# Inputs laid out in reading order, shift and scale columns summed on VectorE, and a first block by k-tiles

## The chip, the cores and the metric

The kernel runs on one core of a Trainium2 chip. The core has five engines that work side by side, each in the order of its own instruction list: TensorE for matrix products (PE in the profile; PEld is its weight load), VectorE (DVE), ScalarE (ACT), GpSimd (POOL) and SyncE (SP), which here only issues transfers. Data come from device memory (HBM) by DMA into the on-chip memory SBUF; matrix products are written to PSUM. The metric is the device time of one execution in microseconds.

## The reference

The program is a small conditioned decoder with two layers on a sequence of 256 positions of width 1024. Each layer is a feed-forward half step, an attention, and another feed-forward half step. In front of every sub-layer stands a normalisation with a shift and a scale, and behind it a gate, that all come from the vector `c`. Cut to what matters here:

```python
c_act = silu(c)
for layer in range(2):
    mods = c_act @ ada_w[layer] + ada_b[layer]          # (1024) x (1024, 9216)
    sh1, sc1, g1, sh2, sc2, g2, sh3, sc3, g3 = split(mods, 9)
    h = rms_norm(x, norm_g[layer, 0]) * (1 + sc1) + sh1
    x = x + 0.5 * g1 * ((silu(h @ w_gate) * (h @ w_up)) @ w_down)    # 1024 -> 2816 -> 1024
    h = rms_norm(x, norm_g[layer, 1]) * (1 + sc2) + sh2
    x = x + g2 * attention(h)             # layer 0: moba, layer 1: mla with its own pair "kv"
    h = rms_norm(x, norm_g[layer, 2]) * (1 + sc3) + sh3
    x = x + 0.5 * g3 * swiglu(h, ...)
```

There are 20 vectors of 1024 from `c` that serve as shift, scale or gate of the two layers and of the pair "kv". Each is a product of `c_act` with a 1024 x 1024 matrix of 4 MB. All data are float32.

## The kernel before, in words

The 256 positions are two tiles `t` of 128 partitions; the width 1024 is eight k-tiles of 128. For a matrix product the normalised `x` is transposed on PE, so that the width lies on the partitions. A shift or scale is then one number per partition, a column of `m_cols`; a gate is wanted along the free dimension, as a row repeated on all partitions.

**Products.** Almost every product is made of three, in a faster format (`mm3`, L695 to L697): both operands are split into a rounded part and a rest, `hi` by ACT (L505) and `lo` by DVE (L506), 1024 columns at a time. A weight tile `raw` of 1 MB (three buffers) is loaded by SP (`wload`, L673), split into `hi` and `lo` (eight buffers each), and its buffer is free when both have read it. Rows of a transfer are as the weights lie in memory: 1 KB for tiles of gate and up, 2 KB for down.

**Vectors from c.** 18 of the 20 vectors are streamed beside the rest (`ada_vec`): eight tiles `adaw` of 128 rows and 1024 columns each (three buffers, L517), and for each tile DVE multiplies with a number per partition and adds into `acc` (L518). POOL clears `acc` beforehand and loads the bias into its row 0. In the end `acc` has to be summed over its 128 partitions. For a gate that is a product with ones (L537, L538). For a shift or scale (12 vectors) `col_sums` transposes `acc` on PE, four blocks of 128 into one PSUM bank `adaps` (L529), and DVE reduces the bank along its rows into four columns (L564); for a scale one more small DVE instruction adds 1 and multiplies the gain (L558). How far the stream runs is set by paces: five vectors are issued during the first feed-forward, one in the first attention, six in the second feed-forward, five in the third, one in the last.

**First block.** The first two vectors, shift and scale of the first sub-layer, are needed at once, so `first` makes the first 512 columns of gate and up with unsplit float32 products (L1527) while the vectors arrive. It works in five rounds of 128, 256, 256, 256 and 128 columns of the vectors. A round loads both vectors' columns for all eight k-tiles (L1445) and the weights of its one or two k-tiles (L1454), forms the columns (round 0 by 32 small products on PE, the others by DVE accumulation, L1488, and products with ones), scales and shifts the transposed `x` on ACT and does the products. The split form of the result is kept for the other blocks.

**Order.** The program is first written down in a sequence with waits for the dependencies; then the class `Order` plays it through with a cost for each instruction and sets each engine's order by need, with numbers for the transfer rate and latency (`RATE`, and the two sums with 1400 and 300 ns). PE's instructions on `adaps` go ahead of others there. On the chip each engine runs its list strictly in that order, and an instruction whose data are late holds all behind it. `first_rank` gives ranks for the first block; `held` keeps some side work (tables for the attention bias) back until 34 us.

Of the kernel before, what the change touches and what calls it, by code (L numbers as in the profile page):

```python
# [68 lines left out]
FFN_PACE = 172.0  # L69

ROUNDS = (128, 256, 256, 256, 128)

INS = ["x", "c", "positions", "ada_w", "ada_b", "norm_g", "ffn_w_gate", "ffn_w_up",
       "ffn_w_down", "rel_bias", "moba_w_qkv", "moba_q_g", "moba_k_g", "moba_w_o",
       "kv_ada_w", "kv_ada_b", "kv_norm_g", "w_dkv", "kv_a_norm_g", "w_uk", "w_uv",
       "mla_k_g", "mla_w_dq", "mla_q_a_norm_g", "mla_w_uq", "mla_q_g", "mla_w_o"]
# [13 lines left out]
RATE = 392.0  # L90
# [55 lines left out]
class Order:  # L146
# [114 lines left out]
    def place(self, need):  # L261
# [70 lines left out]
        while placed < n:  # L332
# [86 lines left out]
def trunk(ctx: ExitStack, tc: tile.TileContext, a: dict, out: bass.AP):  # L419
# [69 lines left out]
    c_rows = tp.tile([P, 256], F32, tag="y", name="c_rows", bufs=4)[:KD, :P]  # L489
    nc.sync.dma_start(c_rows, a["c"].rearrange("o (k p) -> (o k) p", p=P))  # L490
    cact = cp.tile([P, KD], F32, name="cact")
    pos_f = a["positions"].rearrange("o s -> (o s)")
    for t in range(NT):
        nc.scalar.dma_start(xs[t], a["x"][0, t * P:(t + 1) * P, :])
    NGAIN = 7 * KD
    NROW = NGAIN + 2 * KD
    g_rows = cp.tile([P, P], F32, name="g_rows")
    g_cols = cp.tile([P, NROW], F32, name="g_cols")
    m_cols = cp.tile([P, 2, NGAIN], F32, name="m_cols")

# [8 lines left out]
    def ada_vec(w, b, col, finish, rows):  # L509


        acc = adap.tile([P, D], F32, tag="acc", name=nm("acc"), bufs=2)
        nc.gpsimd.memset(acc, 0.0)  # L513
        nc.gpsimd.dma_start(acc[0:1, :], b[col:col + D].rearrange("(o n) -> o n", o=1))
        for k in range(KD):
            wt = adap.tile([P, D], F32, tag="adaw", name=nm("adaw"))
            nc.sync.dma_start(wt, w[k * P:(k + 1) * P, col:col + D])  # L517
            nc.vector.scalar_tensor_tensor(acc, wt, cact[:, k:k + 1], acc,  # L518
                                           op0=ALU.mult, op1=ALU.add)
            if k < KD - 1:  # L520
                yield
        if rows:
            ahi, alo = split(acc, D)

        def col_sums():
            for hh in range(2):
                pt = ps_ada.tile([P, 512], F32, tag="ada", name=nm("adaps"))
                for j in range(4):
                    nc.tensor.transpose(kslice(pt, j), kslice(acc, 4 * hh + j), ident)  # L529
                pe(0.44)  # L530
                finish(hh, pt)

        def sums():
            for hh in range(2):
                pt = ps_ada.tile([P, 512], F32, tag="ada", name=nm("adaps"))
                sl = slice(hh * 512, (hh + 1) * 512)
                nc.tensor.matmul(pt, ones_r, ahi[:, sl], start=True, stop=False)  # L537
                nc.tensor.matmul(pt, ones_r, alo[:, sl], start=False, stop=True)  # L538
                pe(0.44)
                finish(hh, pt)  # L540
        later(3.0, sums if rows else col_sums)
        yield

    mods = {}
    ready = set()

    def mod(*key):
        until(lambda: key in ready)
        return mods.get(key)

    MOD_KEYS = [(0, 0), (0, 1), (0, 2), (1, 0), (1, 1), (1, 2), "kv"]

    def col_slice(t, key, k0=0, n=KD):
        c0 = MOD_KEYS.index(key) * KD + k0
        return t[:, c0:c0 + n]

    def scale_col(ps, key, k0=0, n=KD):
        nc.vector.scalar_tensor_tensor(col_slice(m_cols[:, 1, :], key, k0, n), ps, 1.0,  # L558
                col_slice(g_cols, key, k0, n), op0=ALU.add, op1=ALU.mult)

    def col_fin(key, i):
        def fin(hh, pt):
            s = small([P, 4], "acol") if i else col_slice(m_cols[:, 0, :], key, 4 * hh, 4)
            nc.vector.tensor_reduce(s, pt.rearrange("p (k q) -> p k q", q=P), axis=AX.X, op=ALU.add)  # L564
            if i:
                scale_col(s, key, 4 * hh, 4)
            if hh:
                ready.add((key, ("sh", "sc")[i]))
        return fin

    def gate_fin(key, mul):
        t = mods[key, "g"] = modp.tile([P, D], F32, tag="gate", name=nm("gate"))

        def fin(hh, pt):
            nc.scalar.activation(t[:, hh * 512:(hh + 1) * 512], pt, AF.Copy, scale=mul)
            if hh:
                ready.add((key, "g"))
        return fin

    def ada_items():  # L580
        for layer in range(2):
            w, b = a["ada_w"][layer], a["ada_b"][layer]
            for sub in range(3):
                if layer == 1 and sub == 1:
                    yield a["kv_ada_w"], a["kv_ada_b"], 0, lambda: col_fin("kv", 0), False
                    yield a["kv_ada_w"], a["kv_ada_b"], D, lambda: col_fin("kv", 1), False
                key = (layer, sub)
                if key != (0, 0):
                    yield w, b, 3 * sub * D, lambda key=key: col_fin(key, 0), False
                    yield w, b, (3 * sub + 1) * D, lambda key=key: col_fin(key, 1), False  # L590
                yield (w, b, (3 * sub + 2) * D,
                       lambda key=key: gate_fin(key, 1.0 if key[1] == 1 else 0.5), True)

    def ada_stream():
        for w, b, col, fin, rows in ada_items():
            yield from ada_vec(w, b, col, fin(), rows)
# [21 lines left out]
    def wsrcs():  # L618
        for layer in range(2):
            for idx in range(2):  # L620
                wg, wu, wd = (a[n][layer, idx] for n in ("ffn_w_gate", "ffn_w_up", "ffn_w_down"))
                if (layer, idx) != (0, 0):
                    for w in (wg, wu):
                        for k0 in range(0, KD, 4):
                            yield w[k0 * P:(k0 + 4) * P, :FB], 4, FB
                for f0 in range(FB, F, S):
                    for w in (wg, wu):
                        yield w[:, f0:f0 + S], KD, S
                for half in range(2):
                    for k0 in range(0, KF, 4):  # L630
                        kt = min(4, KF - k0)
                        yield wd[k0 * P:(k0 + kt) * P, half * 512:(half + 1) * 512], kt, 512
                if idx == 1:
                    continue
                if layer == 0:
                    wqkv = a["moba_w_qkv"][0]
                    for g in (0, -1, 1, 2, -2, 3):
# [953 lines left out]
```

## Time and profile before

| what | us |
|---|---|
| median of three runs | 1100.16 |
| lowest and highest run | 1097.55, 1102.19 |
| profiled execution | 1093.43 |
| its span from the first to the last instruction | 1091.7 |
| PE, DVE, ACT busy in the span | 1030.6, 810.1, 583.1 |
| moved by DMA | 260.66 MB, 239 GB/s in the mean |

In the lines of the profile, times are microseconds and `L529` is a line of the kernel. A group of instructions is given as line, engine, operation, result<-operands with their shapes, a count, then the time busy in total and the mean of one in nanoseconds, and then how long the engine stood idle just before them and what ended that. A wait is given as engine and line that waited, what it waited for, the total time, the number of waits and the longest. A line of the timeline is start, duration, engine, line, operation; in square brackets stands the idle time before it. "issue" is a wait that the profile couldn't assign. The duration of an instruction contains the time in which its result travels, so that the next one can start before the end; what one instruction costs its engine is the distance of two starts.

### The profile page before, as it was taken

What the parts mean: (1) busy time and instruction counts of PE and PEld (TensorE: products, weight loads), DVE (VectorE), ACT (ScalarE), POOL (GpSimd) and SP (SyncE); (2) the same over time, 40 slices, a digit from 0 to 9 for tenths busy, and PEclk for the clock granted to TensorE, in tenths of its full rate; (3) what the DMA queues carried; (4) which work ended last, traced back from release to release, by engine and by line L of the source; (5) the groups of instructions that cost most, each with busy time, mean ns of one, the idle gap of its engine ahead of it and who ended that gap; (6) DMA issues with size and microseconds to landing.
All of it is one profiled execution on the core that took longest, in us unless ns stands there. A gap on an engine that the chain in (4) does not pass through costs nothing.

```text
span 1091.7 us, 17404 instructions
## 1 busy us (share of the span) xinstructions
PE 1030.6 (94%) x6692; PEld 906.3 (83%) x6692; DVE 810.1 (74%) x1217; ACT 583.1 (53%) x1054; POOL 97.3 (9%) x155
## 2 busy tenths in 40 slices
PE   7998999988999997999999899999989999999998
PEld 4487899866888787999777799988878878999986
DVE  4798988988976758887998965684589985565542
ACT  4364444337765783435426554543488867555531
POOL 3201100011221001001001000000023200000000
PEclk9998999999999999999999999999999999999999
DMA  9998999989975357997999976475445455555450
GB/s 312 296 306 255 364 333 330 333 278 323 317 256 177 117 161 262 307 321 240 371 324 354 302 224 212 160 243 184 135 131 207 146 184 174 182 169 195 159 191 19
DMA packets 168787, 260.66 MB, mean 239 GB/s; under 512 B 7844, under 2 KB 112084, under 8 KB 168704
## 3 DMA queue, kind: packets, MB, share of 16 engines
q1 hardware_dynamic: 165808, 254.70, 69.2%
q0 software_dynamic: 1552, 3.44, 0.9%
q10 hardware_dynamic: 1344, 1.41, 0.4%
q8 instruction: 52, 0.85, 0.3%
q14 instruction: 31, 0.25, 0.1%
HBM read 255.33 MB, written 4.19 MB: 238 GB/s over the span
## 4 chain that ended last, share of the span: by engine, by line
PE 58%; DVE 15%; DMA 12%; issue 11%; ACT 3%; POOL 1%; SPq 1%; DVEq 0%; ACTq 0%; POOLq 0%
PE mm L697 17%; PE mm L696 17%; PE mm L695 17%; DMA adaw<-in_ada_w_dram 6%; DVE lo L506 5%; DVE acc L518 4%; DMA raw<-in_ffn_w_gate_dram 1%; PE mm L1527 1%; PE at L911 1%; ACT hi L505 1%; DMA bias_d<-bt 1%; DMA acc<-in_ada_b_dram 1%; DVE oh L1091 1%; PE adaps L1496 1%; DMA adaw<-in_kv_ada_w_dram 1%
## 5 line engine op out<-in xcount | busy, mean ns | idle before, releaser
L506 DVE TENSOR_TENSOR lo<-raw,hi 128x1024 fp32r<-128x1024 f32 (+2 forms) x316 | 375.8, 1203 | 85.8 <-ACT hi L505 85.1
L505 ACT ACTIVATE hi<-raw 128x1024 fp32r<-128x1024 f32 (+2 forms) x316 | 324.2, 1040 | 195.6 <-PE mm L697 127.1
L695 PE MATMUL mm<-hh,hi 128*128 128x256 f32 x1152 | 327.8, 286 | 1.7 <-ACT hi L505 1.7
L696 PE MATMUL mm<-hl,hi 128*128 128x256 f32 x1152 | 327.7, 285 | 0.0
L697 PE MATMUL mm<-hh,lo 128*128 128x256 f32 x1152 | 326.0, 285 | 0.2 <-DVE lo L506 0.2
L695 PEld LDWEIGHTS mm<-hh,hi 128*128 128x128 f32 x1152 | 219.8, 191 | 2.5 <-ACT hi L505 1.9
L518 DVE SCALAR_TENSOR_TENSOR acc<-adaw,cact,acc 128x1024 f32<-128x1024 f32 x144 | 184.1, 1279 | 50.2 <-DMA adaw<-in_ada_w_dram 34.8
L696 PEld LDWEIGHTS mm<-hl,hi 128*128 128x128 f32 x1152 | 220.3, 191 | 0.6 <-issue 0.2
L697 PEld LDWEIGHTS mm<-hh,lo 128*128 128x128 f32 x1152 | 219.8, 191 | 0.7 <-DVE lo L506 0.3
L696 PE MATMUL mm<-lo,gh 128*128 128x512 f32 x352 | 137.6, 391 | 0.0
L695 PE MATMUL mm<-hi,gh 128*128 128x512 f32 x352 | 137.2, 392 | 0.0
L697 PE MATMUL mm<-hi,gl 128*128 128x512 f32 x352 | 137.1, 390 | 0.0
L695 PE MATMUL mm<-hi,hh 128*128 128x512 f32 (+1 forms) x240 | 95.4, 403 | 3.4 <-ACT hh L710 3.4
L697 PE MATMUL mm<-hi,hl 128*128 128x512 f32 (+1 forms) x240 | 93.9, 396 | 3.4 <-DVE hl L711 3.2
L696 PE MATMUL mm<-lo,hh 128*128 128x512 f32 (+1 forms) x240 | 93.3, 392 | 2.0 <-DVE lo L506 2.0
L710 ACT ACTIVATE gh<-g 128x256 fp32r<-128x256 f32 x72 | 29.9, 416 | 90.6 <-DVE g L861 85.3
L697 PEld LDWEIGHTS mm<-hi,gl 128*128 128x128 f32 x352 | 66.1, 188 | 13.5
L695 PEld LDWEIGHTS mm<-hi,gh 128*128 128x128 f32 x352 | 66.1, 188 | 13.4
L696 PEld LDWEIGHTS mm<-lo,gh 128*128 128x128 f32 x352 | 66.2, 188 | 13.1
L860 ACT ACTIVATE g<-mm 128x256 f32<-128x256 f32 x72 | 27.1, 376 | 87.8 <-PE mm L697 74.2
L861 DVE TENSOR_TENSOR g<-mm,g 128x256 f32<-128x256 f32 x72 | 30.2, 419 | 45.7 <-ACT g L860 45.7
L513 POOL MEMSET acc<- 128x1024 f32 x18 | 17.2, 955 | 470.1 <-DVE lo L506 275.7
(222 smaller groups left out, 1181.6 us busy)
## 6 DMA issues: line engine op xcount, KB each, us to landing
adaw<-in_ada_w_dram SPq DMA_DIRECT2D x128, 512.0 KB, 6.2
raw<-in_ffn_w_gate_dram SPq DMA_DIRECT2D x42, 1024.0 KB, 6.5
raw<-in_ffn_w_up_dram SPq DMA_DIRECT2D x42, 1024.0 KB, 7.1
raw<-in_ffn_w_down_dram SPq DMA_DIRECT2D x40, 1024.0 KB, 6.2
adaw<-in_ada_w_dram SPq DMA_DIRECT2D x32, 256.0 KB, 6.7
raw<-in_moba_w_qkv_dram SPq DMA_DIRECT2D x16, 512.0 KB, 6.6
adaw<-in_kv_ada_w_dram SPq DMA_DIRECT2D x16, 512.0 KB, 7.0
raw<-in_ffn_w_down_dram SPq DMA_DIRECT2D x8, 512.0 KB, 3.5
```

Source lines behind the costliest of these rows:

```text
L505: nc.scalar.activation(hi, src, AF.Copy)
L506: nc.vector.tensor_tensor(lo, src, hi.bitcast(F32), op=ALU.subtract)
L513: nc.gpsimd.memset(acc, 0.0)
L518: nc.vector.scalar_tensor_tensor(acc, wt, cact[:, k:k + 1], acc, op0=ALU.mult, op1=ALU.add)
L695: nc.tensor.matmul(ps, lh, rh, start=start, stop=False)
L696: nc.tensor.matmul(ps, lh, rl, start=False, stop=False)
L697: nc.tensor.matmul(ps, ll, rh, start=False, stop=stop)
L710: nc.scalar.activation(hi, ps, AF.Copy)
L860: nc.scalar.activation(g, ps[:, 0], AF.Silu)
L861: nc.vector.tensor_tensor(g, ps[:, 1], g, op=ALU.mult)
L911: nc.tensor.matmul(ps3[:, i, :], qTs(e, t), kTs(e, nk), start=bias is not None, stop=bias is not None or i == len(es) - 1)
L1091: V.tensor_scalar(oh[:, i], posq[:, kb * P:], key[:, kb, 8 * c + i:8 * c + i + 1], None, op0=ALU.is_ge)
```

## The change

Three things change together, and the planner's numbers for transfers with them.

1. The inputs are laid out anew before the launch. All weight tiles stand in one array `w` in the order in which they are read, each tile so that a partition's part is contiguous (8 KB). The 20 matrices of the vectors stand in `ada` as eight tiles each; those for shifts and scales are transposed, so that a tile has 128 of the results on its partitions and the 1024 factors along its row. Biases, gains and `c` come as columns in one small table `cols`.
2. `c_act` is repeated on all partitions (`c_b`). A tile of a shift or scale is then done by a single DVE instruction: multiply with `c_b` and add along the row, starting from the bias, with the result as a column. There is no accumulator, no transpose and no reduction. Gates stay as they were, with one accumulator buffer instead of two.
3. The first block goes by k-tiles instead of rounds of columns: for each of the eight, two tiles of vectors, then the k-tile's weights, two DVE instructions for the columns, scaling and shift on DVE for both `t` at once, eight recorded half-products on PE and the split.

```diff
-RATE = 392.0
+RATE = 330.0
...
-                dma_free = max(dma_free, t + 1400.0) + self.transfer(k)
-                dur = dma_free + 300.0 - t
+                dma_free = max(dma_free, t + 1700.0) + self.transfer(k)
+                dur = dma_free + 850.0 - t
...
+def lay_out(v):
+    def tiled(w, kt):
+        return w.reshape(kt, P, -1).transpose(1, 0, 2).reshape(-1)
+    out = {"w": np.concatenate([
+        tiled(np.concatenate([v[n][at][k0 * P:(k0 + kt) * P, c:c + cols] for n, at, c in parts], axis=1), kt)
+        for parts, k0, kt, cols in weight_tiles()])}
...
+        mats.append((w if i == 2 else w.T).reshape(KD, P, D))
...
+    def column(key, i, k, wt):
+        c = NORMS.index(key) * KD + k
+        nc.vector.tensor_tensor_reduce(wt, wt, c_b, 1.0, cols[:, i, c:c + 1], op0=ALU.mult, op1=ALU.add,
+                                       accum_out=m_cols[:, i, c:c + 1])
...
-        acc = adap.tile([P, D], F32, tag="acc", name=nm("acc"), bufs=2)
-        nc.gpsimd.memset(acc, 0.0)
-        nc.gpsimd.dma_start(acc[0:1, :], b[col:col + D].rearrange("(o n) -> o n", o=1))
+    def ada_tile(j, k):
+        wt = adap.tile([P, D], F32, tag="adaw", name=nm("adaw"))
+        nc.sync.dma_start(wt, a["ada"][j, k])
+        return wt
+
+    def ada_cols(j, key, i):
         for k in range(KD):
-            wt = adap.tile([P, D], F32, tag="adaw", name=nm("adaw"))
-            nc.sync.dma_start(wt, w[k * P:(k + 1) * P, col:col + D])
-            nc.vector.scalar_tensor_tensor(acc, wt, cact[:, k:k + 1], acc,
-                                           op0=ALU.mult, op1=ALU.add)
+            column(key, i, k, ada_tile(j, k))
             if k < KD - 1:
                 yield
-        def col_sums():
-            for hh in range(2):
-                pt = ps_ada.tile([P, 512], F32, tag="ada", name=nm("adaps"))
-                for j in range(4):
-                    nc.tensor.transpose(kslice(pt, j), kslice(acc, 4 * hh + j), ident)
-                pe(0.44)
-                finish(hh, pt)
...
-            nc.vector.tensor_reduce(s, pt.rearrange("p (k q) -> p k q", q=P), axis=AX.X, op=ALU.add)
+        if i:
+            scale_col(key)
...
-        for i, sr in enumerate(srcs):
-            dst = rows[:, :, i * m:(i + 1) * m] if isinstance(src, tuple) else rows[:, i * n:(i + 1) * n, :]
-            nc.sync.dma_start(dst, sr.rearrange("(k p) f -> p k f", p=P))
+        n = P * kt * cols
+        nc.sync.dma_start(raw, a["w"][wpos[0]:wpos[0] + n].rearrange("(p f) -> p f", p=P))
...
+        with ranked(0):
+            nc.sync.dma_start(c_b[0:1, :], a["c"])
+            nc.sync.dma_start(cols, a["cols"])
...
+        for k in range(KD):
+            with ranked(2 * k + 2):
                 for i in range(2):
+                    nc.sync.dma_start(wt[k][i], a["ada"][i, k])
+            if k:
+                with ranked(2 * k + 3):
+                    load_w(k - 1)
...
+            nc.scalar.activation(c_b[0:1, :], c_b[0:1, :], AF.Silu)
+            for i in range(2):
+                pt = tr_tile()
+                half = slice(i * 512, (i + 1) * 512)
+                nc.tensor.matmul(pt, ones[0:1, :], c_b[0:1, half], start=True, stop=True)
+                nc.scalar.activation(c_b[:, half], pt, AF.Copy)
...
+        for k in range(KD):
+            with ranked(2 * k + 2):
+                for i in range(2):
+                    column(key, i, k, wt[k][i])
+                scale_col(key, k, 1)
+                z = tp.tile([P, S], F32, tag="y", name=nm("z"), bufs=4)
+                nc.vector.tensor_scalar(z, xT[k // 4][:, k % 4 * S:(k % 4 + 1) * S], col_slice(1, key, k, 1), col_slice(0, key, k, 1),
+                                        op0=ALU.mult, op1=ALU.add)
             for t in range(NT):
+                for i in range(2):
+                    nc.tensor.matmul(accs[t][i], kslice(z, t), raws[k // 2][:, k % 2, i * FB:(i + 1) * FB],
+                                     start=k == 0, stop=k == KD - 1)
+            hi, lo = [x[:, :, k * P:(k + 1) * P] for x in h0[0][3]]
+            split_evac(hi, lo, z.rearrange("p (t q) -> p t q", q=P))
```

More of the change, by code (lines that the diff above doesn't have):

```diff
@@ new lines, in ada_cols, with ada_gate @@
+        ready.add((key, ("sh", "sc")[i]))
+        yield
+    def ada_gate(j, key, row):
+        acc = adap.tile([P, D], F32, tag="acc", name=nm("acc"), bufs=1)
+        nc.gpsimd.memset(acc, 0.0)
+        nc.gpsimd.dma_start(acc[0:1, :], a["rows"][row:row + 1, :])
+        for k in range(KD):
+            nc.vector.scalar_tensor_tensor(acc, ada_tile(j, k), cact[:, k:k + 1], acc, op0=ALU.mult, op1=ALU.add)
+            if k < KD - 1:
+                yield
+        ahi, alo = split(acc, D)
+        t = mods[key, "g"] = modp.tile([P, D], F32, tag="gate", name=nm("gate"))
```

349 lines of the change are left out of this document (135 added, 214 removed).

## The prediction

> **What bounds the kernel now.** I read the page first, then the waits of PE, then the busy time by stage, then single stretches of the timeline.
>
> ```profile
> span 1091.7 us, 17404 instructions
> PE 1030.6 (94%) x6692; PEld 906.3 (83%) x6692; DVE 810.1 (74%) x1217; ACT 583.1 (53%) x1054; POOL 97.3 (9%) x155
> PE 58%; DVE 15%; DMA 12%; issue 11%; ACT 3%; POOL 1%; SPq 1%; DVEq 0%; ACTq 0%; POOLq 0%
> ```
>
> PE is busy for 1030.6 of 1091.7 us, so a gain can only be PE work that goes, or part of its 61.1 us of idle time. The chain that ended last spends 27% in DVE and DMA, more than the idle share: somewhere PE is held by work that other engines deliver. The view of PE's waits names the place:
>
> ```profile
> PE adaps L529 <- issue: 13.0, 7, 3.1
> PE adaps L529 <- DVE m_cols L564: 5.2, 5, 2.6
> PE adaps L529 <- DVE acc L518: 2.6, 1, 2.6
> ```
>
> Together 13.0 + 5.2 + 2.6 = 20.8 us, a third of PE's idle time, stand before the transposes of the column sums (L529). One case shows why:
>
> ```profile
> 130.06 1.28 DVE L518 SCALAR_TENSOR_TENSOR acc<-adaw,cact,acc 128x1024 f32<-128x1024 f32 x1 [0.39 <-DMA adaw<-in_ada_w_dram]
> 131.38 1.28 DVE L518 SCALAR_TENSOR_TENSOR acc<-adaw,cact,acc 128x1024 f32<-128x1024 f32 x1
> 132.72 0.66 PE L529 MATMUL adaps<-ident,acc 128*128 128x128 f32 x4 [2.59 <-DVE acc L518]
> 225.97 0.66 PE L529 MATMUL adaps<-ident,acc 128*128 128x128 f32 x4 [1.41 <-DVE m_cols L564]
> 226.38 0.48 PE L696 MATMUL mm<-lo,gh 128*128 128x512 f32 x1
> ```
>
> The transposes were placed on PE for a time at which the accumulation should have been finished. Its weights landed late, DVE was late, and PE, which runs in order, stood 2.59 us with ready matrix products queued behind. By stage (columns: PE, PEld, DVE, ACT, POOL busy, granted clock, DMA share, GB/s):
>
> ```profile
> 0.00:60.00 60.00, 48.24 (x169) 28.39 (x169) 36.56 (x93) 24.29 (x61) 15.82 (x77) 0.97 0.97 306
> 60.00:256.00 196.00, 181.89 (x1441) 167.61 (x1442) 176.78 (x258) 92.23 (x167) 15.22 (x15) 0.98 0.92 316
> 376.00:590.00 214.00, 201.92 (x1316) 182.02 (x1315) 177.66 (x203) 106.59 (x163) 14.21 (x19) 0.99 0.83 287
> 590.00:790.00 200.00, 193.24 (x1271) 175.45 (x1269) 129.25 (x155) 100.04 (x152) 5.35 (x6) 1.00 0.65 213
> ```
>
> The first 60 us are bound by transfers (share 0.97). The first feed-forward (60 to 256) has DVE at 90% and DMA at 92%, the second (376 to 590) DVE at 83%, the third (590 to 790) neither near its limit.
>
> **The change part by part.**
>
> *Column sums off PE.* 12 of the 18 streamed vectors are columns. For each go 8 transposes, two reductions on DVE, a POOL memset and a small POOL load; POOL is at 9%, so the last two cost nothing.
>
> ```profile
> L529 PE MATMUL adaps<-ident,acc 128*128 128x128 f32 x96 | 15.6, 287 | 20.9 <-issue 13.0 <-DVE m_cols L564 5.2 <-DVE acc L518 2.6
> L564 DVE TENSOR_REDUCE m_cols<-adaps 128x4 f32<-128x512 f32 x12 | 8.2, 683 | 0.0
> L564 DVE TENSOR_REDUCE acol<-adaps 128x4 f32<-128x512 f32 x12 | 8.2, 682 | 0.0
> L518 DVE SCALAR_TENSOR_TENSOR acc<-adaw,cact,acc 128x1024 f32<-128x1024 f32 x144 | 184.1, 1279 | 50.2 <-DMA adaw<-in_ada_w_dram 34.8
> ```
>
> Four transposes hold PE for 226.38 - 225.97 = 0.41 us, so 24 groups hold it 9.8 us: that is PE time saved wholly, since PE sets the pace. The wait of 20.8 us goes with them. DVE loses 16.4 us of reductions. Nothing on PE waits for a column any more; a late column now holds only ACT's scale-and-shift at the next normalisation. Its cover is distance: a vector of a stage is due at that stage's end at the earliest.
>
> *96 accumulations become 96 multiply-and-adds along the row,* with a running sum. The kernel has this instruction at other sizes, in the attention (L924); beside it a step of the accumulation and the next instruction:
>
> ```profile
> 285.35 0.28 DVE L924 CUSTOM_DVE_ANT_0 s<-at,bg 128x128 f32<-128x128 f32 x1
> 285.56 0.28 DVE L924 CUSTOM_DVE_ANT_0 s<-at,bg 128x128 f32<-128x128 f32 x1
> 286.43 0.42 DVE L924 CUSTOM_DVE_ANT_0 s<-at,bg 128x256 f32<-128x256 f32 x1
> 286.78 0.42 DVE L924 CUSTOM_DVE_ANT_0 s<-at,bg 128x256 f32<-128x256 f32 x1
> 75.44 1.28 DVE L518 SCALAR_TENSOR_TENSOR acc<-adaw,cact,acc 128x1024 f32<-128x1024 f32 x1
> 76.64 0.42 DVE L861 TENSOR_TENSOR g<-mm,g 128x256 f32<-128x256 f32 x1
> ```
>
> Start to start, 128 columns take 0.21 us and 256 take 0.35, so 1.09 ns a column and 0.07 fixed: an estimate of 1.19 us for 1024, against 76.64 - 75.44 = 1.20 for the old step. No difference, then: DVE's saving stays at 16 us. Both ends: the row's form reads one operand from PSUM, the new one both from SBUF; if that second read cost a cycle of its own, the slope doubles and the step takes 2.3 us (rival below). The old step, also with two f32 operands in SBUF, is the nearest row and shows no doubling, so I take 1.19.
>
> [...]
>
> *Layout.* Each 1 MB weight tile becomes one transfer of 8 KB rows; before, gate and up tiles have 1 KB rows, down tiles 2 KB, the streamed vectors 4 KB. Rates inside bursts, for 670 to 690 us (only 1 KB rows) and 1040 to 1050 (only 2 KB rows), in 40 slices each, and two longer windows with the vectors' 4 KB rows among them:
>
> ```profile
> GB/s 268 377 385 387 317 66 0 0 0 0 0 33 0 0 152 162 291 375 385 387 356 279 342 367 373 371 305 51 0 16 0 0 0 0 0 0 0 63 152 324
> GB/s 393 418 410 418 418 401 393 393 401 115 0 0 0 0 0 0 0 33 82 16 74 238 336 426 401 418 410 418 410 401 369 156 8 0 0 0 0 0 0 115
> 440.00:500.00 60.00, 60.00 (x502) 60.00 (x501) 49.35 (x58) 26.21 (x39) 0.00 (x0) 1.00 0.94 318
> 530.00:590.00 60.00, 56.83 (x259) 45.44 (x257) 56.45 (x62) 24.33 (x33) 5.80 (x7) 1.00 0.96 354
> ```
>
> 385 against 415 GB/s: longer rows move 8% more in a burst, and 354/0.96 against 318/0.94 is 9% in the mean. This buys no time by itself where PE sets the pace; it is what lets the second stage run faster at all, since 440 to 500 has 6% of the DMA engines' time left. Issues on SP fall (0.37 us each, hidden). Bounds: nothing, up to the 8% in the transfer-bound first block.
>
> *First block by k-tiles.* The data stay the same: 1.0 MB of x, 8.4 of vectors, 4.2 of weights, 13.7 MB with the new table. Old end and the stage behind it:
>
> ```profile
> 10.00:40.00 30.00, 28.77 (x101) 16.54 (x101) 20.55 (x43) 11.32 (x33) 5.21 (x40) 1.00 1.08 340
> 42.61 5.40 PE L1527 MATMUL mm<-raw,z 128*128 128x512 f32 x8 [2.10 <-ACT z L758]
> 43.50 0.38 SPq L673 DMA_DIRECT2D raw<-in_ffn_w_gate_dram  x1
> 48.20 7.11 PE L1527 MATMUL mm<-raw,z 128*128 128x512 f32 x16
> 51.91 0.38 SPq L673 DMA_DIRECT2D raw<-in_ffn_w_up_dram  x1
> 59.11 2.00 ACT L505 ACTIVATE hi<-raw 128x1024 fp32r<-128x1024 f32 x2 [4.00 <-DMA raw<-in_ffn_w_up_dram]
> 60.22 0.39 PE L695 MATMUL mm<-hh,hi 128*128 128x256 f32 x1 [1.70 <-ACT hi L505]
> ```
>
> The last products end at 48.20 + 7.11 = 55.3 us. The next up tile was only asked for at 51.91, as its buffer came free late, and PE's split stage starts for good at 60.2; it had done about 3 us of it before, so 57 counts. New: at 340 GB/s (the row) to 385 (4 KB rows) from 3 us on, 13.7 MB have landed at 43 to 39 us. Each k-tile brings 1.57 MB (4.6 to 4.1 us), against 8 half-products of (7.11 - 0.59)/15 = 0.43 us, 3.5 us, on PE and some 3.4 us on DVE (two steps of 1.19, scaling, shift, split): transfers bind both. The last k-tile's vectors come a megabyte ahead of the end, so the block ends some 3.5 us behind it, at 42 to 47. The next gate tile takes the buffer of k-tiles 2 and 3, free long before, lands 3 us behind the last weight and is split between 44 and 49; the up tile follows in time. So the split stage starts at 47 instead of 57: 10 us. Bounds: 14 at 385 GB/s throughout; 3 if DVE's saturated stretch behind it cannot start earlier. The broadcast of c (a load, one activation, two products, two copies) lies beside x's landing. On SP's queue c, the table and x (from ACT's queue) now stand ahead of the vectors: three issues of 0.37 us more, inside the 3 us. The 16 vector tiles fill all 16 split buffers, but each is free after its step, before the gate tile lands. The accumulator's second buffer goes; gates lie two vectors apart, so no one waits for it.
>
> *Order.* The planner's transfer rate drops from 392 to 330 and its latencies grow by 0.3 and 0.55 us, which reorders every engine. The nearest measure is PE's idle time outside the waits named, 40 us: a quarter of it, 10 us, either way. I take zero.
>
> **What is late next.** Without 8.3 us of waits and 3.3 of transposes the stage 60 to 256 wants DVE's 176.8 - 5.5 = 171.3 us in 184: 93%, above any stage now. The second wants 169.5 in 199.6, 85%, but its last stretch, 530 to 590, has DVE at 56.45 of 60 already; the third is free. I let a third of the 20.8 us come back as waits for the splits (L506): 7 us.
>
> Sum: -9.8 - 20.8 + 7 - 10 = -33.6 us on the profiled execution's 1093.4, so 1060. The median of the runs lies 6.7 above that execution: 1066.5.
>
> **The rivals.** *DVE takes over wholly:* the splits hold PE for all that the transposes did, and the start's gain is eaten by the same saturated DVE. For it: DVE at 90% in 60 to 256. Against: the third stage's waits have DVE at 65%. Gain 9.8 and some 3: 1087.
> *Slower: the new step at half rate.* 1.1 us more each. With DVE full to 93% as above, the first stage lasts (171.3 + 24 x 1.1)/0.93 = 213 us, 17 more than before, the second (169.5 + 32 x 1.1)/0.93 = 220, 6 more; the start keeps 6 and the third stage 5 of gain: 12 slower, 1112. It turns at 0.9 us extra, a step of 2.1 us. Against it stands the old step's row. [...]
> *More:* longer rows and the truer planner also take a third of PE's other 40 us: 13 and the 7 not returned, 1047.
> *No change:* every removed wait returns and the start too: 1095 to 1100.
>
> **How the numbers follow.** Forecast (1055 to 1080) 0.52; more 0.14; DVE takes over 0.16; no change 0.06; slower 0.12, of which half rate is 0.08 and an unlucky order 0.04. A measurement of this kernel tells 0.5%, 5.5 us, from no change: faster 0.82, same 0.06, slower 0.12. 1042 to 1094 leaves out some 0.2 and holds the first two bounds of every unknown but the half rate.
>
> **What would show it.** Right: no transposes and no reductions from the vectors' path; PE's idle time near 35 us, with L506 among the releasers; the new step at 1.2 to 1.3 us; the block's products ending near 45 us; bursts above 400 GB/s. Wrong: a step over 2 us; DVE over 95% in the first feed-forward with PE waiting on L506; PE waiting for the gates' sums or for scale-and-shift as it did for the transposes; a first block that ends past 50 us.

## The result, and the profile after

The changed kernel takes 1042.05 us in the median (1040.58 to 1043.66). The kernel before, run in turn with it, takes 1098.86 us. The ratio is 0.9485, with a 95% interval of 0.9448 to 0.9522: 5% faster, some 57 us, where 34 had been forecast. The sign was right, and the gain was two thirds larger than its sum. The time lies below the forecast's 1055 to 1080 us, and within the wider range of 1042 to 1094 by 0.05 us only.

From the page of the changed kernel come its span, the busy time of the engines, the chain of work that ended last, and the row of the new DVE step:

```profile
span 1038.8 us, 16938 instructions
PE 1006.2 (97%) x6538; PEld 884.6 (85%) x6538; DVE 798.1 (77%) x1280; ACT 577.4 (56%) x1031; POOL 85.7 (8%) x128
PE 76%; DVE 12%; DMA 5%; ACT 3%; issue 2%; POOL 2%; SPq 0%; DVEq 0%; POOLq 0%; ACTq 0%
L593 DVE CUSTOM_DVE_ANT_0 adaw<-adaw,c_b,cols 128x1024 f32<-128x1024 f32 x112 | 141.5, 1278 | 1.3 <-DMA adaw<-in_ada_dram 1.3
```

PE's busy time fell by 24.4 us and its idle time from 61.1 to 32.6. In the chain DMA fell from 12% to 5% and "issue" from 11% to 2%: PE had been held by late data. The last number of the row says it again from DVE's side: the new steps waited 1.3 us in all for their tiles, where the old accumulations had waited 34.8 us for one of their sources alone.

PE's longest waits in the changed kernel, beside 3.4 us at its very start for the repeated `c` (engine, line, what it waited for: total, times, longest):

```profile
PE tr L1482 <- ACT y L1480: 4.9, 3, 2.6
PE tr L757 <- ACT y L752: 4.7, 4, 2.2
PE adaps L639 <- ACT hi L582: 2.5, 1, 2.5
```

`adaps` is now written by the gates' sums only (L639, L640). They wait 2.5 us where the transposes had waited 20.8. PE's products wait 0.3 us for the splits of weights; before, it was 3.9, of which these are the longest:

```profile
PE mm L696 <- DVE lo L506: 2.0, 2, 1.0
PE mm L695 <- ACT hi L505: 1.7, 1, 1.7
```

What is left in the changed kernel are mainly the transposes of the normalised x in the first block (L1482) and at the other normalisations (L757).

Where the time went is seen by stage. First the kernel before, then the changed kernel, both cut at about the first split product behind each stage (busy PE, PEld, DVE, ACT, POOL, then granted clock, DMA share, GB/s). For the kernel before, the first cut is at 57 and not at 54.75, since after some 3 us of split products PE stood again until 60.2. The stages are the first block, the first, second and third feed-forward; the attention between the first two feed-forwards, and all that follows the third, are left out.

```profile
0.00:57.00 57.00, 46.72 (x158) 27.09 (x159) 34.09 (x82) 23.40 (x60) 15.82 (x77) 0.97 0.97 304
57.00:256.70 199.70, 183.94 (x1457) 169.10 (x1456) 179.95 (x270) 93.79 (x169) 15.49 (x16) 0.98 0.92 316
379.00:589.00 210.00, 199.19 (x1304) 180.74 (x1304) 173.76 (x197) 102.73 (x155) 13.65 (x18) 0.99 0.84 291
589.00:792.00 203.00, 195.94 (x1285) 177.62 (x1282) 132.25 (x160) 103.04 (x158) 5.35 (x6) 1.00 0.66 214
```

```profile
0.00:50.00 50.00, 39.33 (x86) 17.04 (x87) 32.01 (x72) 17.71 (x37) 13.93 (x72) 0.97 0.92 342
50.00:233.60 183.60, 178.84 (x1438) 165.64 (x1436) 165.60 (x280) 94.09 (x169) 10.09 (x9) 1.00 0.88 315
355.00:546.50 191.50, 190.85 (x1256) 174.80 (x1256) 168.57 (x223) 103.08 (x155) 6.03 (x6) 1.00 0.89 326
546.50:737.00 190.50, 190.20 (x1256) 174.60 (x1256) 125.75 (x163) 99.98 (x151) 3.56 (x4) 1.00 0.62 218
```

The start gave 7.0 us, the three feed-forwards 16.1, 18.5 and 12.5, the rest together lost 1.2: 52.9 us of span. In the second and third feed-forward PE is now busy for all but 0.65 and 0.3 us. The third, in which neither DVE nor DMA is near a limit, gained 12.5 us all the same: 6.8 of idle time and 5.7 of PE's work. So the gain is not that of a relieved engine alone. Something late had held PE there too.

### The profile page after: what moved, and what is told of

It reads as the page before. It is cut to its first block, busy times and chain, and to the rows that moved or that the text cites. A ratio compares the mean times of both kernels' runs of the same rounds, so it can differ in the third digit from the quotient of the medians.

```text
span 1038.8 us, 16938 instructions
## 1 busy us (share of the span) xinstructions
PE 1006.2 (97%) x6538; PEld 884.6 (85%) x6538; DVE 798.1 (77%) x1280; ACT 577.4 (56%) x1031; POOL 85.7 (8%) x128
## 4 chain that ended last, share of the span: by engine, by line
PE 76%; DVE 12%; DMA 5%; ACT 3%; issue 2%; POOL 2%; SPq 0%; DVEq 0%; POOLq 0%; ACTq 0%
PE mm L711 24%; PE mm L709 24%; PE mm L710 24%; DVE lo L583 4%; DMA adaw<-in_ada_dram 2%; DMA raw<-in_first_dram 2%; DVE oh L1105 1%; POOL hr L1017 1%; DVE acc L629 1%; ACT hi L582 1%; PE mm L1494 1%; PE at L925 1%; DMA raw<-in_w_dram 1%; ACT y L772 1%; ACT y L752 1%
## 5 line engine op out<-in xcount | busy, mean ns | idle before, releaser
L593 DVE CUSTOM_DVE_ANT_0 adaw<-adaw,c_b,cols 128x1024 f32<-128x1024 f32 x112 | 141.5, 1278 | 1.3 <-DMA adaw<-in_ada_dram 1.3
L711 PEld LDWEIGHTS mm<-hi,gl 128*128 128x128 f32 x352 | 66.1, 188 | 13.8
L629 DVE SCALAR_TENSOR_TENSOR acc<-adaw,cols,acc 128x1024 f32<-128x1024 f32 x48 | 61.3, 1278 | 0.8 <-DMA adaw<-in_ada_dram 0.6
L709 PEld LDWEIGHTS mm<-hi,hh 128*128 128x128 f32 x240 | 45.1, 188 | 12.0 <-ACT hh L724 3.7
```

The source lines that it names most:

```text
L593: nc.vector.tensor_tensor_reduce(wt, wt, c_b, 1.0, cols[:, i, c:c + 1], op0=ALU.mult, op1=ALU.add, accum_out=m_cols[:, i, c:c + 1])
L629: nc.vector.scalar_tensor_tensor(acc, ada_tile(j, k), cact[:, k:k + 1], acc, op0=ALU.mult, op1=ALU.add)
L709: nc.tensor.matmul(ps, lh, rh, start=start, stop=False)
L711: nc.tensor.matmul(ps, ll, rh, start=False, stop=stop)
```

## The experiments

Every kernel here computes the whole reference; work that is added leaves results that nobody reads. "After" is the changed kernel. Each was timed in turn with the kernel before, whose medians in the three sets were 1098.25, 1099.48 and 1098.83 us. A difference from the changed kernel is one of medians, with 1042.05 for it; it joins runs of different sets, between which the medians of the kernel before differ by up to 1.2 us.

**First set: which part brings it.** The rivals were: the gain is that of the transposes (their work and the waits before them), or of the layout, or of the planner's numbers.

*The transposes back, with the wait.* Into the changed kernel come eight transposes per streamed column vector again, of a small tile that the last DVE step of the vector fills, so that PE has to wait for it as before.

```diff
+        nc.vector.tensor_copy(probe[:, :1], m_cols[:, i, c:c + 1])
+        def sums():
+            for hh in range(2):
+                ...
+                for q in range(4):
+                    nc.tensor.transpose(kslice(pt, q)[:64], probe, ident)
+        later(3.0, sums)
```

> The new kernel with 8 transposes put back on PE behind every streamed shift or scale vector, each waiting for that vector's last DVE step (a 64-column probe tile that DVE writes one column of stands in for the old accumulator; the transposes' results are not used). Theory A (PE was held by transposes that wait for late vectors): 12 us for the work (24 groups of 0.41 to 0.49 us) and 10 to 20 us of waits come back: 1064 to 1074 us. Rival B (the waits came from late weights, i.e. from the old row lengths, or from the old planner numbers): the work alone comes back, 1052 to 1056 us.

*The transposes back, without the wait.* The same, but of `c_b`, which is ready from the first microseconds on.

```diff
+                    nc.tensor.transpose(kslice(pt, q), kslice(c_b, 4 * hh + q), ident)
```

> The same transposes, but of data that are ready all along (the repeated c), so without any wait. Theory A and rival B alike: the work alone, 24 groups of 0.41 to 0.49 us, 10 to 12 us: 1052 to 1054 us. The difference to the run with the waits is the price of the waits.

Measured: 1049.47 us with the wait (ratio to the kernel before 0.9534, 0.949 to 0.9578) and 1052.29 without it (0.9562, 0.9518 to 0.9606). The transposes' work is worth 10.2 us, as forecast (9.8). The wait is worth nothing: the kernel whose transposes depend on the vector is no slower than the one whose transposes do not (the blocks of the former are 64 columns wide; what that takes from their work was not measured). Either theory had a longer time for it. No wait of PE in its profile stands before these transposes. So the 20.8 us in front of the transposes were not inherent in them. In the changed kernel DVE is early: it stands for 1.9 us in all in front of tiles of the vectors, and PE for 2.5 us in front of the gates' sums.

*The old layout of the weights.* The changed kernel reads the weight tiles as they lie, with rows of 1 and 2 KB.

```diff
-        nc.sync.dma_start(raw, a["w"][wpos[0]:wpos[0] + n].rearrange("(p f) -> p f", p=P))
+            nc.sync.dma_start(dst, sr.rearrange("(k p) f -> p k f", p=P))
```

> The new kernel, with the weight tiles read from the weights as they lie in memory (rows of 1 KB for gate and up, 2 KB for down), everything else new. Theory A (layout only makes room on the DMA engines, PE sets the pace): 1042 to 1047 us, with the DMA engines' share in the second feed-forward up from 0.89 to 0.95 or more. Rival C (the longer rows are what let the second feed-forward shrink by 19 us): 1052 to 1062 us, with PE waiting for splits there.

Measured: 1041.37 us (0.9461, 0.9418 to 0.9505), no difference that this kernel's times can tell. The same stretch of this kernel as above for the second feed-forward:

```profile
355.00:546.50 191.50, 191.50 (x1251) 175.86 (x1250) 166.63 (x220) 100.61 (x149) 6.03 (x6) 0.99 0.93 324
```

With the short rows the DMA share is 0.93 against 0.89, for the same 324 to 326 GB/s; theory A had said 0.95 or more. By its split products the stage itself lasts from 354.01 to 547.58 us here, 2.3 us more than in the changed kernel (355.25 to 546.51), and its first 6 us ran at half clock (last section). In the time of the whole kernel the layout buys nothing.

*The planner's old numbers.* The changed kernel is ordered with 392, 1400 and 300 again. No instruction is added or removed, the order alone changes.

```diff
-RATE = 330.0
+RATE = 392.0
-                dma_free = max(dma_free, t + 1700.0) + self.transfer(k)
-                dur = dma_free + 850.0 - t
+                dma_free = max(dma_free, t + 1400.0) + self.transfer(k)
+                dur = dma_free + 300.0 - t
```

> The new kernel with the planner's old numbers (392, 1400, 300). Theory A: the numbers move single waits, 1038 to 1048 us. Rival D (the gain beyond the forecast, some 19 us, comes from the truer planner): 1054 to 1062 us.

Measured: 1065.32 us (0.9673, 0.9619 to 0.9727). 23.3 us come from three constants, more than from any part so far and more than rival D had said. The waits of this kernel show where. PE's and DVE's:

```profile
PE adaps L639 <- ACT hi L582: 11.8, 3, 6.3
PE adaps L640 <- DVE lo L583: 4.6, 2, 3.6
DVE adaw L593 <- DMA adaw<-in_ada_dram: 28.9, 23, 2.7
DVE acc L629 <- DMA adaw<-in_ada_dram: 11.7, 10, 2.0
```

DVE stands 40.6 us in front of tiles of the vectors that have not landed. PE then stands 16.4 us in front of the gates' sums, with no transposes of columns anywhere. That is the same kind of wait as before, at the next instruction that needs DVE's vectors: the `hi` and `lo` named here are those of a gate's finished vector.

This gave a new theory: the planner, which assumed 392 GB/s, ordered DVE's list for tiles that land earlier than they do. DVE runs its list in order, so a step whose tile is late holds the splits behind it, and these hold PE. The first half of it can be seen in the kernel before, on ACT and then on DVE:

```profile
186.47 2.94 ACT L505 ACTIVATE hi<-raw 128x1024 fp32r<-128x1024 f32 x3
190.88 1.28 DVE L518 SCALAR_TENSOR_TENSOR acc<-adaw,cact,acc 128x1024 f32<-128x1024 f32 x1 [2.62 <-DMA adaw<-in_ada_w_dram]
192.09 3.49 DVE L506 TENSOR_TENSOR lo<-raw,hi 128x1024 fp32r<-128x1024 f32 x3
```

ACT has done its half of three splits by 189.41; DVE stands for 2.62 us until 190.88, makes the late step, and three splits of its own come behind it, from 192.09 on. If the theory holds, the three constants help the kernel before as well, and taking its transposes away helps it little.

**Second set: the parts on the kernel before, and DVE's room.**

*The kernel before with the new numbers.* The diff above, the other way round, and nothing else.

> The kernel before with the planner's new numbers (330, 1700, 850) and nothing else. Theory A: the transposes still stand on PE and still wait; a truer transfer time in the planner places them later, so some of the 20.8 us goes: 1088 to 1098 us. Rival D (planner): 1075 to 1085 us.

Measured: 1064.34 us (0.9662, 0.9587 to 0.9737), 35 us faster than the kernel before, with all transposes in place, and faster than either theory had it. The waits of DVE in the kernel before, the longest three for tiles and biases of the vectors:

```profile
DVE acc L518 <- DMA adaw<-in_ada_w_dram: 34.8, 22, 4.5
DVE acc L518 <- DMA acc<-in_ada_b_dram: 7.6, 3, 4.3
DVE acc L518 <- DMA adaw<-in_kv_ada_w_dram: 5.6, 4, 2.3
```

and from the kernel with the new numbers the chain of work that ended last, PE's wait before the transposes and DVE's waits for the same three:

```profile
PE 82%; DVE 10%; ACT 2%; issue 2%; DMA 2%; POOL 1%; ACTq 0%; SPq 0%; DVEq 0%; POOLq 0%
PE adaps L529 <- issue: 4.9, 3, 3.5
DVE acc L518 <- DMA adaw<-in_ada_w_dram: 4.9, 5, 2.7
DVE acc L518 <- DMA adaw<-in_kv_ada_w_dram: 1.0, 2, 0.5
DVE acc L518 <- DMA acc<-in_ada_b_dram: 0.9, 1, 0.9
```

DVE's 48.0 us became 6.8, the 20.8 us before the transposes became 4.9, and DMA and "issue" went from 23% of the chain to 4%. The transposes are the same 96 instructions. One link of the theory is not borne out: PE's products had stood for the splits of weights for only 3.9 us. Late tiles held PE mainly through the vectors, whose sums stand in PE's list.

*The columns alone.* The kernel before with the columns by multiply-and-add, and its old weight layout, old first block and old numbers.

```diff
-        def col_sums():
-            ...
-                    nc.tensor.transpose(kslice(pt, j), kslice(acc, 4 * hh + j), ident)
+            column(key, i, k, ada_tile(j, k))
```

> The second part alone: columns by multiply-and-add along the row, no transposes or reductions; weights as they lie in memory, the first block in five rounds of columns and the planner's numbers as before. The matrices of shifts and scales have to be transposed for it, the streamed tiles of all vectors keep rows of 4 KB. Theory A: 12 us of PE work and 15 to 21 us of waits go, 1066 to 1073 us. Rivals C and D: the waits turn up elsewhere, since rows and planner are the old ones, and only the work goes: 1085 to 1088 us.

Measured: 1096.49 us (0.9959, 0.9922 to 0.9997). The part that names the change, taken alone, gives 0.4%, not even the 10 us of the transposes' work, and less than either theory had said. Its waits:

```profile
PE adaps L640 <- ACT hi L583: 21.1, 3, 10.1
DVE adaw L594 <- DMA adaw<-in_ada_dram: 29.1, 22, 3.1
DVE acc L630 <- DMA adaw<-in_ada_dram: 14.6, 11, 2.7
DVE acc L630 <- DMA acc<-in_rows_dram: 4.3, 1, 4.3
```

Three waits of PE before the gates' sums, 21.1 us, stand in the place of the 20.8 us before the transposes, and DVE waits for late tiles and a bias for 48.0 us, as it had before. Two more things take from the gain. The first block's products end at 57.3 us, 2.0 later than before, and the repetition of `c` on all partitions stands behind them on PE for 1.98 us. And PE's busy time fell by 4.0 us only (1026.6 against 1030.6), with its mean granted clock at 0.981 against 0.993.

*The old first block.* The changed kernel with the five rounds of before.

```diff
-        for k in range(KD):
-            with ranked(2 * k + 2):
-                for i in range(2):
-                    column(key, i, k, wt[k][i])
+        for j in range(len(ROUNDS)):
+            with ranked(j):
+                load_ada(j)
+                load_w(j)
```

> The new kernel with the old first block (five rounds of columns, 0.5 to 1 KB rows for the vectors, column sums by DVE accumulation and PE; biases and gains from the new table). In the profiles the block's last products ended at 55.3 us before and 50.0 us after. Theory A, first block worth that difference: 1046 to 1050 us. The forecast's 10 us: 1052 us. Rival: DVE, saturated behind the block, hides it: 1042 us.

Measured: 1051.43 us (0.955, 0.9488 to 0.9612): undoing the first block by k-tiles costs 9.4 us, near the forecast's 10 and above theory A. It is not quite the kernel before's block that comes back. Its last products:

```profile
54.85 3.70 PE L1536 MATMUL mm<-raw,z 128*128 128x512 f32 x8 [1.18 <-ACT z L775]
```

They end at 58.6 us, 3.2 later than in the kernel before, and the repetition of `c` follows on PE (1.98 us). In the kernel before with the new numbers alone, too, they end at 57.6. Under the new numbers the old block is slower than it was. Against the kernel before, the products of the change's block end only 5.3 us earlier; that block alone on the kernel before was not run.

*DVE's room.* In the changed kernel each of the 96 streamed steps is done twice, the second time into a column that nobody reads.

```diff
+            nc.vector.tensor_tensor_reduce(wt, wt, c_b, 1.0, cols[:, i, :1], op0=ALU.mult, op1=ALU.add,
+                                           accum_out=junk_col)
```

> The new kernel with the multiply-and-add along the row done twice for each of the 96 streamed tiles (the second result is thrown away): 115 us more DVE work, spread as 24, 8, 32 and 32 over the first feed-forward, the first attention, the second and the third feed-forward. It prices a step at twice its time. Theory A with the forecast's rule (a stage can be filled to 93% with DVE work): 25 us in the first and 31 us in the second feed-forward, 1095 to 1100 us. If DVE can be filled to 98%: 1080 to 1085 us. If DVE had room: 1042 us.

Measured: 1047.88 us (0.9518, 0.9457 to 0.9579), between the theory with room and the two without. 96 steps more, 104.5 us of DVE's busy time, cost 5.8 us. The busy line of this kernel and one line of DVE's waits, and then the same line of the changed kernel with what ACT's half of the splits waits for there:

```profile
PE 1010.5 (97%) x6538; PEld 888.2 (85%) x6538; DVE 902.6 (86%) x1472; ACT 579.7 (55%) x1031; POOL 90.5 (9%) x128
DVE lo L584 <- ACT hi L583: 42.0, 56, 5.8
```

```profile
DVE lo L583 <- ACT hi L582: 120.2, 160, 5.6
ACT hi L582 <- PE mm L711: 125.8, 87, 7.1
ACT hi L582 <- PE mm L710: 30.3, 67, 0.9
ACT hi L582 <- DMA raw<-in_w_dram: 9.8, 4, 4.0
```

DVE had been waiting in front of splits for ACT's half, 120.2 us in all, and ACT in turn mostly for PE to finish products (156.1 us) and only 9.8 us for weights: the splits were ahead of PE. 78 us of DVE's waits went when the new steps came. A stage with DVE at 90% did not yet hold PE back.

**Third set: which number, and what is still left.**

*The rate alone*, and *the latencies alone*, on the kernel before:

```diff
-RATE = 392.0
+RATE = 330.0
```

> The kernel before with the planner's transfer rate alone changed (392 to 330), latencies 1400 and 300 as before. Theory E (formed on the runs so far: DVE's list was written for transfers that land earlier than they do, so DVE stands in front of late vector tiles, 54 us in all before and 8 us with all three new numbers, with ready splits queued behind): the rate is the larger part, since the rate inside the streamed stages decides when a tile queued behind others lands: 1070 to 1080 us. Rival F (the fixed latencies are what the planner lacked): 1090 to 1100 us.

```diff
-                dma_free = max(dma_free, t + 1400.0) + self.transfer(k)
-                dur = dma_free + 300.0 - t
+                dma_free = max(dma_free, t + 1700.0) + self.transfer(k)
+                dur = dma_free + 850.0 - t
```

> The kernel before with the planner's latencies alone changed (1400 and 300 to 1700 and 850), rate 392 as before. Theory E with the rate as the larger part: 1085 to 1097 us. Rival F: 1064 to 1075 us.

Measured: 1069.68 us (0.9731, 0.9699 to 0.9763) and 1094.73 us (0.996, 0.9937 to 0.9983). Of the 35 us the rate alone brings 29 and the latencies alone 4, as theory E had it.

*The first block's end.* In the changed kernel the last products of the first block end at 41.16 + 8.80 = 50.0 us, later than forecast. From its timeline SP's load of the last weights, PE's last products and the first split product, and SP's wait ahead of such a load (L1444):

```profile
34.22 5.85 SPq L1444 DMA_DIRECT2D raw<-in_first_dram  x2
41.16 8.80 PE L1494 MATMUL mm<-raw,z 128*128 128x512 f32 x16 [1.93 <-DMA raw<-in_first_dram]
49.39 0.68 PE L709 MATMUL mm<-hh,hi 128*128 128x256 f32 x1
```

```profile
SPq L1444 <- DMA gpek<-in_mla_k_g_dram: 5.2, 1, 5.2
```

SP stood for 5.2 us, and it was waiting for a small table of the last attention, `gpek`, which the planner had put beside the first block. The table is among those that `held` keeps back until 34 us, just when the last weights are to be asked for. The experiment holds these constants back until 130 us instead:

```diff
-                    hold(mla_consts)
+                    hold(mla_consts, 130e3)
```

> The new kernel with the small loads of the last attention's constants (gains and the shared part, issued on ACT's queue at 33 to 35 us) held back in the planner from 34 to 130 us. In the new kernel's profile SP waits 5.2 us for one of these loads before it issues the last weights of the first block, and PE then stands 1.9 us and runs at about half clock for 2 to 3 us. Theory: the block's last products end at 45 instead of 50 us and the end comes 3 to 5 us earlier: 1037 to 1039 us. Rival (the saturated DVE behind the block hides it): 1042 us.

Measured: 1038.62 us (0.9448, 0.9419 to 0.9477), as the theory had it and 3.4 us less than the changed kernel, whose fastest run (1040.58) is above the slowest of this one (1039.39). Its last products:

```profile
39.02 7.11 PE L1494 MATMUL mm<-raw,z 128*128 128x512 f32 x16 [0.30 <-DMA raw<-in_first_dram]
```

They end at 46.1 us, 3.8 earlier, about the gain. That the load was held by these constants is shown by their removal; which of them did it, and why SP has to wait for one instead of issuing ahead, wasn't settled.

*Slower still in the plan.* The same, with numbers beyond those of the change: 300 GB/s, 2000 and 1400 ns.

```diff
-RATE = 330.0
+RATE = 300.0
-                dma_free = max(dma_free, t + 1700.0) + self.transfer(k)
-                dur = dma_free + 850.0 - t
+                dma_free = max(dma_free, t + 2000.0) + self.transfer(k)
+                dur = dma_free + 1400.0 - t
```

> The same, with still more pessimistic planner numbers (rate 300, latencies 2000 and 1400). Theory E: in the new kernel DVE waits only 1.9 us for tiles, so there is little left to gain: within 4 us of the run without it. Rival (more margin always helps): 5 us or more faster.

Measured: 1037.62 us (0.9442, 0.9418 to 0.9467), the fastest version found, but, as theory E had it, only by 1.0 us and with overlapping intervals: beyond 330 the number has little more to give.

Put together: 35.1 us for the planner's numbers (on the kernel before, 1099.48 to 1064.34), and, each undone in the changed kernel, 10.2 for the transposes' work, 9.4 for the first block, nothing for the layout. That is 54.7 of the 56.8 us that were measured, but it is no clean sum: in the changed kernel the numbers are worth 23.3, and taken alone on the kernel before, the columns are worth 3.0. The 2.1 us that are left are not assigned. What the columns save shows only once the order is right.

## Why the prediction was right in sign and wrong in size

The sum was -9.8 for the transposes' work, -20.8 + 7 for their wait, -10 for the first block and zero for the order. The experiments give 10.2 and 9.4 for the first and the third. In the place of the wait and the order together, 13.8 us of gain, stand 35 for the order. That the time still fell within the wide range, at its very edge, is luck: the largest cause was put at nothing, and its effect on one wait was credited to another part.

**The order: the step that failed.** "I take zero", with 10 us either way. It measured 35 us on the kernel before and 23.3 on the changed one. The bound was taken from PE's idle time outside the waits named, as if the named waits could not be the planner's. They were. The row for it stood in the prediction: the accumulations (L518) sat idle for 50.2 us, 34.8 of them for DMA, which was read only for its mean duration. So did the rows for the number itself: 340 GB/s from 10 to 40 us and 354 from 530 to 590, at DMA shares of 1.08 and 0.96, where the planner counted on 392, 11 to 15% more. A plan that is too fast places DVE's steps, and the sums on PE that need their vectors, before the tiles have landed.

**"The wait of 20.8 us goes with them."** This failed too, and it hid the first failure. The 20.8 us were put down to the transposes, as PE stood in front of them. With the columns alone they moved to the gates' sums, 21.1 us; with the planner's numbers alone most of them went, transposes and all. The prediction named "PE waiting for the gates' sums … as it did for the transposes" as a sign that it was wrong, and on the columns alone that sign came. The cause was upstream on DVE, and the waiting instruction was only the first to need it.

**The transposes' work,** 9.8 us: right, 10.2.

**A third of the wait returns, 7 us:** wrong, nothing returned. The stage was forecast to want DVE at 93% in 184 us, and it took 183.6 with DVE at 90%. PE's products waited 0.3 us for splits of weights. The doubled steps show why the limit was no limit: 104.5 us more of DVE's work cost 5.8.

**The first block,** 10 us: right in size, 9.4. Its way was not the one forecast. The products should have ended at 42 to 47 and ended at 50.0, just short of the prediction's own sign of being wrong, because of a load held on SP's queue, which the prediction had not foreseen. Without that hold they end at 46.1, and the kernel gains 3.4 us more. So the 9.4 us agree with the 10 in part by luck: against the kernel before, the products end 5.3 us earlier and the start is 7.0 shorter, and the old block under the new numbers was slower than it had been.

**The layout:** "buys no time by itself" was right, "what lets the second stage run faster at all" was wrong: with the short rows the stage takes 193.6 us, part of it from a half clock at its start, against 191.3, and both are far below the 210 of the kernel before. Rates above 400 GB/s came in the first block; in the first two feed-forwards the mean is 315 and 326. The forecast's 385 GB/s for rows of 4 KB was read from bursts with rows of 1 KB. In the first block of the changed kernel, where the rows of vectors and weights have 4 KB, five of the seven stretches of 4 us between 4 and 32 us moved 405 to 416 GB/s, the other two 314 and 320.

**The new step:** 1.19 us forecast, start to start. The timeline of the changed kernel shows a step and the reading of its sum:

```profile
17.41 1.28 DVE L593 CUSTOM_DVE_ANT_0 adaw<-adaw,c_b,cols 128x1024 f32<-128x1024 f32 x1
18.61 0.08 DVE L593 DVE_READ_ACCUMULATOR2_ANT m_cols<- 128x1 f32 x1
```

18.61 - 17.41 = 1.20 us. The rival with the half rate, and the slower kernel that it would have made, fell with this row. Its step of 2.3 us was the author's estimate, for a second read that doubles the time of a column. No run shows such a step: all 112 instructions of the new form, with both operands in SBUF, take 1278 ns in the mean, as the old form without an accumulated sum did (1279).

**The rivals.** "More", 1047 us, came nearest and had the right mechanism among its two, the truer planner, at some third of its size. "DVE takes over wholly" and "no change" rested on DVE having no room, which it had.

## What to carry to other kernels

A wait belongs to what is late, and the engine that stands in front of it is only where it shows: before a wait is credited to the instruction that is removed, follow it up one engine, and ask what the next instruction in need of the same data would do. Where the order is fixed beforehand by a plan, compare the plan's transfer rate with the rate in the trace; here a constant 11 to 15% above it cost 29 us of 1099, more than any piece of work that the change removed. Test parts alone and undone: the columns alone gained 3.0 us, and their transposes put back into the changed kernel cost 10.

## What the runs showed of the hardware

At three places shown here a short stand of PE was followed by a half clock, in which its products took longer; at a fourth it was not. Four stretches of the changed kernel around the last products of the first block (PE, PEld, DVE, ACT, POOL busy, then the granted clock), and the same place in the kernel that holds the constants back:

```profile
38.00:40.00 2.00, 1.23 (x3) 0.19 (x1) 1.88 (x5) 0.00 (x0) 0.00 (x0) 1.00 0.54 205
40.00:42.00 2.00, 0.84 (x2) 0.49 (x3) 1.41 (x4) 0.42 (x1) 0.00 (x0) 1.00 0.63 156
42.00:44.00 2.00, 2.00 (x4) 0.86 (x3) 0.30 (x1) 0.00 (x0) 0.00 (x0) 0.61 1.03 432
44.00:46.00 2.00, 2.00 (x4) 0.74 (x3) 0.00 (x0) 0.13 (x1) 0.00 (x0) 0.53 1.00 412
```

```profile
44.00:46.00 2.00, 2.00 (x6) 0.81 (x6) 2.00 (x4) 1.77 (x3) 0.00 (x0) 1.00 1.04 418
```

After a wait of 1.93 us, with PE busy for 2.07 us of the four from 38 to 42, its clock was at half for some 3.4 us, and the 16 products took 8.80 us where they took 7.11 with a wait of 0.30 in front. The kernel before shows the same in its first feed-forward, behind a wait of 1.54 us:

```profile
90.00:92.00 2.00, 1.71 (x24) 1.30 (x24) 2.00 (x9) 0.00 (x0) 0.00 (x0) 0.72 0.74 184
92.00:94.00 2.00, 1.11 (x18) 1.05 (x18) 2.00 (x9) 0.00 (x0) 0.00 (x0) 0.50 0.95 337
```

Here the half clock lasted some 6.8 us, from 90.9 to 97.7, and a second wait of 0.99 us fell into it; split products of 256 columns started 0.21 us apart in it and 0.12 us apart behind it. The same stand did not always cost the same. In front of the second feed-forward the changed kernel and the one with the old layout of the weights have the same waits, 2.15 us before six transposes and 0.70 us behind them; the second and third product that follow, in this order:

```profile
355.59 0.39 PE L710 MATMUL mm<-lo,hh 128*128 128x512 f32 x1
355.82 0.40 PE L709 MATMUL mm<-hi,hh 128*128 128x512 f32 x1
```

```profile
354.60 0.63 PE L752 MATMUL mm<-lo,hh 128*128 128x512 f32 x1
355.03 0.63 PE L751 MATMUL mm<-hi,hh 128*128 128x512 f32 x1
```

The first kernel kept its clock of 1.00; the second ran at half from 353.4 to 360.1, some 6.7 us. What decides between the two is not shown.

Of the time that removing late data gained, a part is therefore clock. The changed kernel and the same kernel with the planner's old numbers have the same 6538 instructions on PE; in their profiles PE is busy for 1006.2 us at a mean granted clock of 0.998 and for 1015.0 us at 0.986.
